# The S5 mixer of a two-layer trunk in straight line: paired gelu, tables prepared earlier, first gated columns in native fp32

## The chip, the cores and the metric

The kernel runs on one core of a Trainium2 chip. The metric is the device time of one execution in microseconds; the median of several runs counts.

## The reference, cut to what matters

Two layers over 256 tokens of 2048 channels. Layer 0 is differential attention and an MLP with squared ReLU, layer 1 an S5 state space mixer with a gated output (GLU), and an MLP; a norm ends it. Only the S5 mixer is touched, and the last two matrix products of the first MLP run beside steps that are moved.

```python
def s5_mixer(h, ...):                      # h: rmsnorm(x) * gain, 256 x 2048
    u = h.reshape(B, S, S5_GROUPS, S5_GROUP)
    bu_re = einsum('sgc,gpc->sgp', u_s, bb_re); bu_im = ...
    x_re, x_im = associative_scan(_scan_combine, (a_re, a_im, bu_re, bu_im))
    y = einsum('sgp,gcp->sgc', x_re, cr) - einsum('sgp,gcp->sgc', x_im, ci)
    y = y + d_skip * h
    g = gelu(y)
    val, gate = split(g @ w_glu, 2, axis=-1)    # w_glu: 2048 x 4096
    return val * sigmoid(gate)
```

## The kernel before, in words

All matrix products with weights run on TensorE in the fp32r type, with both operands split in two parts: `wh` is the weight cast by ScalarE (`prep`, L173), `wl` the remainder by VectorE or GpSimd (L99, L178, L179), and each product takes three matmuls, h x h, h x l, l x h (L186 to L188, `ktile`). Weights come in chunks of 512 KB (two 128-deep slices, 512 columns) on the queue of SyncE (SP), `load`, five buffers (`raw`); `prep` of chunk i also loads chunk i + 5. An output block is 512 columns wide and takes eight chunks.

Side work is written as generators. `pump` advances every generator that is due, once after each 128-deep slice of a main matrix product; `spawn` adds one. The order in which the Python code issues is the order of each engine's queue; the engines wait for one another by semaphores. A tile with a tag takes the buffer of that tag that was freed first.

The S5 mixer works on 16 tiles of 128 channels, four tokens to a chunk, so that a tile has 4 x 64 columns. Per tile j there is a table in DRAM, `scr[j]`, 1.5 MB, made from the weights beside the first layer (`s5_pre`), and these steps:

- `s5_u` (two tiles): TensorE transposes the residual (L940), ScalarE copies it in 16 pieces of 32x128 into u (L945); `s5_scale` multiplies by the norm's factor per token (L951, GpSimd; VectorE for the first pair).
- `s5_fetch`: three loads of 512 KB, `te`, `to` and `t` (L926 to L928), for j < 3 on SP's queue, after that on ScalarE's, and a copy of the decay `rr` on ScalarE (L930).
- `s5_e`: state inputs, 16 fp32 matmuls (32 records in the trace, L961), then a chain on VectorE: two multiplications by the turn, an add and a subtraction, two scans (L971), two multiplications back, a subtraction for the real half; the add for the imaginary half runs on GpSimd for j < 10 (L983).
- `s5_y`: outputs, 24 fp32 matmuls (48 records, L994), then 16 gelus of 32x64 on ScalarE (L999).
- `s5_split`: the cast of the gelu's result (ScalarE, L1010) and the remainder (L1011, GpSimd for j < 10).

`s5_run` is the generator that issues them, tile after tile, with `keep_warm` matmuls that nobody reads (L269) at its start. The main stream meanwhile multiplies the first 512 columns of value and gate (`a_v`, `a_g`, `gemm_block`): per tile twelve fp32r matmuls of 512 columns, as soon as the tile is split. Chunks 384 to 399 (GLU0 = 384) are those weights; they are cast and split like all the others. Then follow the other three column blocks, `gemm(glu_lhs)`. `early_u` makes u of tiles 0 to 3 and fetches tables 0 and 1 beside the last three products of the first MLP; `done0` starts it after the first of four last products, and `gemm_skewed` is the last of them.

Of the kernel before, what the change touches and what calls it, by code (L numbers as in the profile page):

```python
# [16 lines left out]
P = 128  # L17
S = 256
# [38 lines left out]
def tile_trunk(  # L57
# [104 lines left out]

    def prep(i):
        if i >= len(stream) or i in preps:
            return
# [5 lines left out]
        for k in range(0, WK, step):  # L171
            sl = slice(k, k + step)
            act.copy(h[:, sl], r[:, sl])  # L173
            if FINE <= i < POOL or GLU0 <= i < GLU0 + 16:
                if i < GLU0 or i >= GLU0 + 2:
                    sub(l[:, 0], r[:, 0], h[:, 0].bitcast(F32))
                else:
                    pool_e.tensor_tensor(out=l[:, 0], in0=r[:, 0], in1=h[:, 0].bitcast(F32), op=ALU.subtract)  # L178
# [15 lines left out]
    def gemm_block(accs, lhs, first, last, ks=range(KB)):  # L194
        """accumulate one weight block (512 deep, 512 wide) or a part of it for both token tiles"""
# [22 lines left out]
    def gemm_t(lhs_blocks):  # L218
        """as gemm, but the result transposed: weights stationary, tokens moving"""
# [22 lines left out]
    def gemm_skewed(lhs_blocks, done):  # L242
        """the last half of the depth one token tile after the other"""
# [19 lines left out]
    def keep_warm(n):  # L263
        """matmuls whose result nobody reads: TensorE's clock drops when it idles"""
# [86 lines left out]
    class Norm:  # L351
        """rms statistics of the residual, a block of columns at a time"""
# [15 lines left out]
        def finish(self, ts=slice(0, NT)):  # L368
            """1/sqrt(mean square + eps), or its square"""
# [78 lines left out]
    def evict_qk(hp, accs, which):  # L448
        """queries unscaled (their norm factor enters the softmax), keys with theirs"""
# [9 lines left out]
    def head(hp, hh):  # L459
        """scores, softmax, difference; waits for v; values, sub-norm, transposed output"""  # L460
# [117 lines left out]
    def s5_pre():  # L578
# [10 lines left out]
        # lambda and step in the layout [(group of pair, state), pair]  # L589
# [660 lines left out]
```

## Time and profile before

| | us |
|---|---|
| median of 3 runs | 2154.13 (2153.45 to 2154.57) |
| profiled execution, span from first to last instruction | 2150.9 |
| TensorE busy | 2098.5 (98%) |
| VectorE busy | 1340.2 (62%) |
| ScalarE busy | 1088.6 (51%) |
| GpSimd busy | 178.3 (8%) |

Of the profiled execution only the span is given; its time is not among the three. PE is TensorE, PEld its weight loads, DVE VectorE, ACT ScalarE, POOL GpSimd, SP SyncE. A busy TensorE is not TensorE at its peak, and matmul records overlap: spacing of starts says more than durations. A native fp32 matmul leaves two records.

### The profile page before, as it was taken

Reading aid. Unit: us, or ns where it says so; the run is one execution under the profiler, and the core shown is the slowest. Engines: PE = TensorE matmul, PEld = TensorE weight load, DVE = VectorE, ACT = ScalarE, POOL = GpSimd, SP = SyncE. Lnnn points to the kernel's source line nnn. Section 1 sums busy time; section 2 is a strip of 40 time slices with the busy share of each in tenths; the row PEclk is TensorE's granted clock in tenths of the full one; section 3 lists DMA queues with packets and bytes.
Section 4 is the critical chain, followed back from the end, with each engine's and each line's share of the span. In section 5 each row is a group of like instructions: output and inputs, shape, how many; then the busy total and the mean of one; then the engine's idle time right before and its main releaser. Section 6 shows DMA issues by size and latency. Waiting matters only on the chain.

```text
span 2150.9 us, 35993 instructions
## 1 busy us (share of the span) xinstructions
PE 2098.5 (98%) x14210; PEld 1887.1 (88%) x14210; DVE 1340.2 (62%) x2182; ACT 1088.6 (51%) x1685; POOL 178.3 (8%) x279
## 2 busy tenths in 40 slices
PE   8999999999999999999997789999999999999998
PEld 8899988898899899889975568899889989989986
DVE  5775556777677767757766775555555555545555
ACT  5444545555444544544465995454434434434443
POOL 1000200120021012001102520000000000000000
PEclk9999999999999999999999899999999999999999
DMA  7567765788777778776776755666566566566653
GB/s 243 157 199 234 240 182 175 221 235 279 222 233 231 267 223 233 273 238 220 229 248 224 264 183 182 195 197 191 190 193 183 187 194 186 176 199 184 191 191 127
DMA packets 230829, 452.83 MB, mean 211 GB/s; under 512 B 20818, under 2 KB 29348, under 8 KB 230660
## 3 DMA queue, kind: packets, MB, share of 16 engines
q1 hardware_dynamic: 212784, 395.89, 58.9%
q0 software_dynamic: 11440, 32.86, 4.7%
q10 hardware_dynamic: 6436, 21.79, 2.8%
q8 instruction: 111, 1.82, 0.3%
q14 instruction: 58, 0.48, 0.1%
HBM read 420.85 MB, written 41.68 MB: 215 GB/s over the span
## 4 chain that ended last, share of the span: by engine, by line
PE 92%; ACT 3%; DVE 2%; DMA 1%; issue 1%; ACTq 0%; POOL 0%; SPq 0%; DVEq 0%; POOLq 0%
PE acc L186 15%; PE acc L188 15%; PE acc L187 15%; PE acc L233 14%; PE acc L234 14%; PE acc L235 14%; ACT s2k L999 1%; ACT vsb L945 1%; ACT wh L173 1%; PE sd L388 0%; DVE wl L99 0%; DVE c L93 0%; PE sd L961 0%; PE sd L994 0%; DVE s2k L971 0%
## 5 line engine op out<-in xcount | busy, mean ns | idle before, releaser
L99 DVE TENSOR_TENSOR wl<-raw,wh 128x1024 fp32r<-128x1024 f32 (+1 forms) x704 | 851.6, 1215 | 657.3 <-ACT wh L173 651.5
L173 ACT CAST wh<-raw 128x1024 fp32r<-128x1024 f32 (+1 forms) x706 | 735.6, 1046 | 768.5 <-PE acc L188 384.7
L233 PE MATMUL acc<-xh,wh 128*128 128x256 f32 x1536 | 439.9, 286 | 1.2 <-ACT wh L173 1.2
L235 PE MATMUL acc<-xh,wl 128*128 128x256 f32 x1536 | 435.3, 283 | 0.0
L234 PE MATMUL acc<-xl,wh 128*128 128x256 f32 x1536 | 435.3, 283 | 0.0
L186 PE MATMUL acc<-wh,xh 128*128 128x512 f32 x896 | 357.2, 399 | 23.1 <-ACT xh L1010 20.4
L187 PE MATMUL acc<-wl,xh 128*128 128x512 f32 x896 | 352.0, 393 | 0.8 <-POOL wl L178 0.8
L188 PE MATMUL acc<-wh,xl 128*128 128x512 f32 x896 | 352.1, 393 | 0.4 <-DVE xl L1011 0.4
L233 PEld LDWEIGHTS acc<-xh,wh 128*128 128x128 f32 x1536 | 295.3, 192 | 3.4 <-ACT wh L173 1.6
L234 PEld LDWEIGHTS acc<-xl,wh 128*128 128x128 f32 x1536 | 295.4, 192 | 0.4
L235 PEld LDWEIGHTS acc<-xh,wl 128*128 128x128 f32 x1536 | 295.3, 192 | 0.2 <-DVE wl L99 0.2
L233 PE MATMUL acc<-ah,wh 128*128 128x256 f32 x1024 | 289.9, 283 | 0.0
L235 PE MATMUL acc<-ah,wl 128*128 128x256 f32 x1024 | 289.8, 283 | 0.0
L234 PE MATMUL acc<-al,wh 128*128 128x256 f32 x1024 | 289.8, 283 | 0.0
L186 PE MATMUL acc<-wh,ah 128*128 128x512 f32 x640 | 251.6, 393 | 0.4 <-ACT wh L173 0.4
L187 PE MATMUL acc<-wl,ah 128*128 128x512 f32 x640 | 249.4, 390 | 1.4 <-DVE wl L99 1.4
L188 PE MATMUL acc<-wh,al 128*128 128x512 f32 x640 | 249.3, 390 | 0.0
L186 PEld LDWEIGHTS acc<-wh,xh 128*128 128x128 f32 x896 | 169.7, 189 | 58.7 <-ACT xh L1010 21.5
L188 PEld LDWEIGHTS acc<-wh,xl 128*128 128x128 f32 x896 | 169.7, 189 | 38.0 <-POOL bc L980 1.2
L187 PEld LDWEIGHTS acc<-wl,xh 128*128 128x128 f32 x896 | 170.1, 190 | 35.0 <-POOL wl L178 1.2
L234 PEld LDWEIGHTS acc<-al,wh 128*128 128x128 f32 x1024 | 196.6, 192 | 0.2
L233 PEld LDWEIGHTS acc<-ah,wh 128*128 128x128 f32 x1024 | 196.6, 192 | 0.2
(237 smaller groups left out, 1931.6 us busy)
## 6 DMA issues: line engine op xcount, KB each, us to landing
raw<-in_mlp_w_dram SPq DMA_DIRECT2D x512, 512.0 KB
raw<-in_a_w_in_dram SPq DMA_DIRECT2D x94, 512.0 KB
raw<-in_b_w_glu_dram SPq DMA_DIRECT2D x64, 512.0 KB
raw<-in_a_w_out_dram SPq DMA_DIRECT2D x32, 512.0 KB
scr<-t POOLq DMA_DIRECT2D x32, 512.0 KB, 6.0
te<-scr ACTq DMA_DIRECT2D x13, 512.0 KB
to<-scr ACTq DMA_DIRECT2D x13, 512.0 KB
t<-scr ACTq DMA_DIRECT2D x13, 512.0 KB
```

The lines of the kernel that those rows point to most:

```text
L99: v.tensor_tensor(out=o, in0=a, in1=b, op=ALU.subtract)
L173: act.copy(h[:, sl], r[:, sl])
L186: pe.matmul(accs[t], lhs.h[:, k, ts], wh, start=first, stop=False)
L187: pe.matmul(accs[t], lhs.h[:, k, ts], wl, start=False, stop=False)
L188: pe.matmul(accs[t], lhs.l[:, k, ts], wh, start=False, stop=last)
L233: pe.matmul(o, wh[:, kk, cs], lhs.h[:, k], start=f and c % 2 == 0, stop=False)
L234: pe.matmul(o, wh[:, kk, cs], lhs.l[:, k], start=False, stop=False)
L235: pe.matmul(o, wl[:, kk, cs], lhs.h[:, k], start=False, stop=e and c % 2 == 1)
L945: act.copy(u[32 * s:32 * s + 32, :, q], pv[32 * q:32 * q + 32, :, L - 1 - s])
L999: act.activation(gv[32 * q:32 * q + 32, s], py[32 * s:32 * s + 32, q], AF.Gelu_apprx_tanh)
```

## The change

`s5_run`, a generator, becomes `s5_phase`, a straight loop over the 16 tiles; the interleaver runs only the table generator beside it. In iteration j it issues the state inputs of tile j + 1, a decay row of tile j + 3 (now a GpSimd copy, `s5_dk`), a scaling, the GLU step of tile j - 3 (`glu_tile`), the outputs of tile j and, at the end of a pair, 16 gelus of 32x128 for both tiles with one split (`s5_y` over a group; the last two tiles are alone), u of a pair (tiles 8 to 15 only), and the fetch of table j + 4. `glu_tile` multiplies the unsplit gelu by the raw weights, four native fp32 matmuls of 512 columns per tile, so chunks 384 to 399 are not cast nor split. All tables are fetched on SP's queue. The add of the imaginary half and the remainder are on GpSimd for all tiles. u of tiles 4 to 7 is made in the first MLP, after its second last-quarter product, and `early_tables` fetches tables from there as soon as `s5_pre` is done. Comments are removed elsewhere.

```diff
-S5_POOL = 10
+LAG = 3
     def prep(i):
-        if i >= len(stream) or i in preps:
+        if i >= len(stream) or i in preps or GLU0 <= i < GLU0 + 16:
             return
...
-        load(i + RAW)
+        load_next()
...
     def s5_fetch(j):
-        eng = nc.sync if j < 3 else nc.scalar
-        te = lp.tile([P, 2, Q, P], F32, tag="ah", name=nm("te"))
+        tag = "x" if j < 3 else "a"
+        te = lp.tile([P, 2, Q, P], F32, tag=tag + "h", name=nm("te"))
...
+    def s5_dk(j):
+        dk = tmp([P, Q, NCH], "s1k", bufs=4)
+        pool_e.tensor_copy(dk, rr[:, j * Q:(j + 1) * Q, None].broadcast_to([P, Q, NCH]))
...
+    def s5_y(grp):
...
         for s in range(L):
             for q in range(Q):
-                act.activation(gv[32 * q:32 * q + 32, s], py[32 * s:32 * s + 32, q], AF.Gelu_apprx_tanh)
+                act.activation(gv[32 * q:32 * q + 32, 0:n, s], py[32 * s:32 * s + 32, 0:n, q], AF.Gelu_apprx_tanh)
+        act.copy(blk.h[:, kk:kk + n], g[:, 0:n])
+        pool_e.tensor_tensor(out=blk.l[:, kk:kk + n], in0=g[:, 0:n], in1=blk.h[:, kk:kk + n].bitcast(F32), op=ALU.subtract)
...
+    def glu_tile(j):
+        g = G.pop(j)
+        c, kk = GLU0 + j // WK * 2, j % WK
+        for i, accs in ((c, a_v), (c + 1, a_g)):
+            for t in range(NT):
+                pe.matmul(accs[t], g[:, t * P:(t + 1) * P], raws[i][:, kk], start=j == 0, stop=j == NJ - 1)
+            if j == NJ - 1 and i == c:
+                first_vals.extend(evict_val(a_v))
+            if kk == WK - 1:
+                load_next()
+                pos[0] += 1
+
+    def s5_phase(norm):
+        until(lambda: norm.done)
         keep_warm(WARM[0])
...
         s5_scale(0, rsb, v)
+        for j in range(3):
+            DK[j] = s5_dk(j)
         s5_scale(2, rsb)
         s5_e(0)
+        keep_warm(WARM[2])
...
         for j in range(NJ):
+            if j + 1 < NJ:
+                s5_e(j + 1)
+            if j + 3 < NJ:
+                DK[j + 3] = s5_dk(j + 3)
+            if j % 2 == 0 and j + 4 < NJ and j + 4 in U:
                 s5_scale(j + 4, rsb)
+            if j >= LAG:
+                glu_tile(j - LAG)
+            gen, end = ys[j]
+            next(gen)
...
+            if j % 2 == 1 and j + 7 < NJ:
+                s5_u(j + 7)
+            s5_fetch(j + 4)
+            pump()
+        for j in range(NJ - LAG, NJ):
+            prep(GLU0 + 16 + j - NJ + LAG)
+            glu_tile(j)
...
+        if u < 2:
+            spawn(early_u(u), 4)
         if u == 0:
-            spawn(early_u(), 4)
+            spawn(early_tables(), 2)
...
+    def early_u(u):
+        for j in (4 * u, 4 * u + 2):
+            s5_u(j)
+            yield 4
+
+    def early_tables():
+        while "done" not in s5:
             yield 1
+        for j in range(4):
+            s5_fetch(j)
+            yield 8
+            while j == 2 and pos[0] < last_mlp0 - 2:
+                yield 1
```

## Rows read from the trace of the kernel before

**Rows 1.** Timeline, TensorE: start us, us, engine line op out<-in xcount [idle before].
```profile
1139.79 0.39 PE L188 MATMUL acc<-wh,al 128*128 128x512 f32 x1
1140.02 4.24 PE L269 MATMUL acc<-xh 128*128 128x512 f32 x18
...
1287.19 0.39 PE L186 MATMUL acc<-wh,xh 128*128 128x512 f32 x1
1287.41 0.39 PE L187 MATMUL acc<-wl,xh 128*128 128x512 f32 x1
```
**Rows 2.** Stretches: from:to, us, then each engine's busy us, clock, DMA share, GB/s.
```profile
1160.00:1170.00 10.00, 3.87 (x87) 3.15 (x83) 8.16 (x14) 9.57 (x32) 3.48 (x5) 1.00 0.59 187
1170.00:1180.00 10.00, 5.15 (x55) 3.78 (x55) 6.29 (x9) 9.58 (x35) 3.71 (x6) 0.71 0.56 187
1171.00:1182.30 11.30, 7.18 (x59) 4.98 (x59) 6.22 (x10) 10.94 (x34) 4.80 (x8) 0.65 0.57 189
1182.30:1196.00 13.70, 11.63 (x183) 9.48 (x182) 13.16 (x17) 13.01 (x44) 10.18 (x12) 0.92 0.88 299
1190.00:1285.00 95.00, 75.77 (x1004) 57.90 (x1001) 72.27 (x120) 89.55 (x289) 34.76 (x47) 0.93 0.65 221
```
**Rows 3.** Chain of waits from 1070 to 1300, its shares by line.
```profile
by line: ACT s2k L999 13.2%; PE acc L186 11.3%; PE acc L188 10.7%; PE acc L187 10.5%; ACT vsb L945 10.0%; issue 8.0%; ACT wh L173 3.5%; DVE c L93 3.4%; PE sd L961 3.3%; PE sd L994 3.2%; DVE s2k L971 3.2%; DVE s2k L93 3.0%; DMA t<-bbr 2.8%; 
```
**Rows 4.** Groups of ScalarE from 1140 to 1287, by form: busy us, mean ns, idle before.
```profile
L999 ACT ACTIVATE s2k<-sd 32x64 f32<-32x64 f32 x256 | 71.5, 279 | 11.9 <-PE sd L994 8.8
L945 ACT COPY vsb<-sd 32x128 f32<-32x128 f32 x96 | 24.7, 257 | 1.2
L173 ACT CAST wh<-raw 128x1024 fp32r<-128x1024 f32 x19 | 19.6, 1043 | 0.0
L1010 ACT CAST xh<-s2k 128x256 fp32r<-128x256 f32 x16 | 6.5, 405 | 0.4
L930 ACT COPY s1k<-rr 128x256 f32<-128x256 f32 x14 | 5.6, 400 | 3.0 <-PE sd L1025 2.8 <-issue 0.2
```
**Rows 5.** Timeline of ScalarE, the same step of two pairs of tiles.
```profile
1223.30 4.66 ACT L999 ACTIVATE s2k<-sd 32x64 f32<-32x64 f32 x16
...
1240.31 4.64 ACT L999 ACTIVATE s2k<-sd 32x64 f32<-32x64 f32 x16
```
**Rows 6.** Timeline of TensorE at an attention head: native fp32, 256 columns.
```profile
90.53 0.60 PE L512 MATMUL sd<-vsb,s2k 128*128 128x256 f32 x2
90.96 0.59 PE L513 MATMUL sd<-vsb,s2k 128*128 128x256 f32 x2
91.39 0.59 PE L514 MATMUL sd<-vsb,s2k 128*128 128x256 f32 x2
```
**Rows 7.** Timeline and chain: state inputs and outputs of S5 on TensorE.
```profile
1145.94 2.08 PE L961 MATMUL sd<-vsb,te 128*64 128x64 f32 x64
1154.70 1.15 PE L961 MATMUL sd<-vsb,te 128*64 128x64 f32 x32
1182.33 1.98 PE L961 MATMUL sd<-vsb,te 128*64 128x64 f32 x32
1255.38 1.55 PE sd L994 x48
```
**Rows 8.** Timeline of VectorE and GpSimd, the first tiles of S5.
```profile
1147.13 1.29 DVE L93 TENSOR_TENSOR c<-sd,t 128x512 f32<-128x512 f32 x2 [1.29 <-PE sd L961]
1152.08 1.28 DVE L93 TENSOR_TENSOR c<-sd,t 128x512 f32<-128x512 f32 x2
1157.02 1.28 DVE L93 TENSOR_TENSOR c<-sd,t 128x512 f32<-128x512 f32 x2
1161.96 1.28 DVE L93 TENSOR_TENSOR c<-sd,t 128x512 f32<-128x512 f32 x2
1163.29 1.54 POOL L951 TENSOR_TENSOR vsb<-vsb,rsb 128x512 f32<-128x512 f32 x1 [0.66 <-ACT vsb L945]
1163.62 1.50 DVE L99 TENSOR_TENSOR c<-c 128x256 f32<-128x256 f32 x1
1165.04 1.26 DVE L971 TENSOR_TENSOR_SCAN s2k<-s1k,c 128x256 f32<-128x256 f32 x2
```
**Rows 9.** Groups of GpSimd and VectorE from 1140 to 1287, by form.
```profile
L951 POOL TENSOR_TENSOR vsb<-vsb,rsb 128x512 f32<-128x512 f32 x7 | 10.6, 1517 | 20.4 <-DVE rsb L1027 19.8 <-ACT vsb L945 0.7
L983 POOL TENSOR_TENSOR bc<-s2k,s2k 128x252 f32<-128x252 f32 x10 | 9.2, 916 | 18.2 <-DVE s2k L93 18.2
L1011 POOL TENSOR_TENSOR xl<-s2k,xh 128x256 fp32r<-128x256 f32 x10 | 8.2, 817 | 39.4 <-ACT xh L1010 39.4
...
L971 DVE TENSOR_TENSOR_SCAN s2k<-s1k,c 128x256 f32<-128x256 f32 x32 | 23.3, 767 | 0.0
```
**Rows 10.** A stretch of the first MLP in which tables 0 and 1 are loaded.
```profile
1126.00:1137.00 11.00, 11.00 (x50) 9.13 (x49) 3.99 (x9) 2.83 (x4) 0.00 (x0) 1.00 0.98 374
```
**Rows 11.** Timeline of TensorE in the first MLP, where u of tiles 0 to 3 is made.
```profile
1086.23 0.50 PE L186 MATMUL acc<-wh,ah 128*128 128x512 f32 x1 [0.36 <-ACT wh L173]
1087.49 0.50 PE L187 MATMUL acc<-wl,ah 128*128 128x512 f32 x1 [0.76 <-DVE wl L99]
...
1093.83 0.50 PE L187 MATMUL acc<-wl,ah 128*128 128x512 f32 x1 [0.60 <-DVE wl L99]
```

More of the change, by code (lines that the diff above doesn't have):

```diff
@@ L173, in prep @@
             act.copy(h[:, sl], r[:, sl])
[L174 to L178, printed above, removed]
+            if FINE <= i < POOL:
+                sub(l[:, 0], r[:, 0], h[:, 0].bitcast(F32))
                 pool_e.tensor_tensor(out=l[:, 1], in0=r[:, 1], in1=h[:, 1].bitcast(F32), op=ALU.subtract)
@@ L980, in s5_e @@
         pool_e.memset(xp[:, :, :, 0:1], 0.0)
-        eng = pool_e if j < S5_POOL else v
         sub(xp[:, 0, :, 1:], w1[:, 0, :, 0:n], w2[:, 1, :, 0:n])
-        eng.tensor_tensor(out=xp[:, 1, :, 1:], in0=w1[:, 1, :, 0:n], in1=w2[:, 0, :, 0:n], op=ALU.add)
+        pool_e.tensor_tensor(out=xp[:, 1, :, 1:], in0=w1[:, 1, :, 0:n], in1=w2[:, 0, :, 0:n], op=ALU.add)
         X[j] = xp
-    def s5_y(j):
-        te, to, tt, ct, dk = tab.pop(j)
-        u, xp = U.pop(j), X.pop(j)
-        py = bank()[:, 0:Q * NCH].rearrange("p (q k) -> p q k", q=Q)
-        for q in range(Q):
-            terms = ((tt[:, q], u[:, q]), (to[:, 0, q], xp[:, 0, q]), (to[:, 1, q], xp[:, 1, q]))
-            for n, (m, d) in enumerate(terms):
-                for h in (slice(0, GP), slice(GP, P)):
-                    pe.matmul(py[h, q], m[:, h], d, start=n == 0, stop=n == 2)
-        g = tmp([P, S], "s2k", bufs=7)
-        gv = g.rearrange("p (k s) -> p s k", s=L)
+    def s5_y(grp):
+        n = len(grp)
+        py = bank().rearrange("p (j q k) -> p j q k", j=2, q=Q)
+        for jj, j in enumerate(grp):
+            te, to, tt, ct = tab[j]
+            u, xp = U[j], X[j]
+            for q in range(Q):
+                terms = ((tt[:, q], u[:, q]), (to[:, 0, q], xp[:, 0, q]), (to[:, 1, q], xp[:, 1, q]))
+                for m, (w_, d) in enumerate(terms):
+                    for h in (slice(0, GP), slice(GP, P)):
+                        pe.matmul(py[h, jj, q], w_[:, h], d, start=m == 0, stop=m == 2)
+            yield j
+            del U[j], X[j], tab[j]
+        g = tmp([P, 2, S], "s2k", bufs=7)
+        gv = g.rearrange("p j (k s) -> p j s k", s=L)
@@ L997, in s5_y @@
         for s in range(L):
             for q in range(Q):
[L999 to L1005 removed]
+                act.activation(gv[32 * q:32 * q + 32, 0:n, s], py[32 * s:32 * s + 32, 0:n, q], AF.Gelu_apprx_tanh)
+        blk, kk = glu_lhs[grp[0] // KB], grp[0] % KB
         if blk.h is None:
             new_lhs(blk, "x")
[L1008 to L1014 removed]
@@ L1016, in s5_run @@
-    def s5_run(norm):
-        while not norm.done:
-            yield 1
+        act.copy(blk.h[:, kk:kk + n], g[:, 0:n])
+        pool_e.tensor_tensor(out=blk.l[:, kk:kk + n], in0=g[:, 0:n], in1=blk.h[:, kk:kk + n].bitcast(F32), op=ALU.subtract)
+        if kk + n == KB:
+            blk.ready = True
+        for jj, j in enumerate(grp):
+            G[j] = g[:, jj]
+    def glu_tile(j):
+        g = G.pop(j)
+        c, kk = GLU0 + j // WK * 2, j % WK
[7 more added lines that the diff above has]
+                pos[0] += 1
@@ L1179, in tile_trunk @@
     a_v, a_g = new_accs(), new_accs()
-    for b in range(NB):
-        for k in range(0, KB, WK):
-            ks = range(k, k + WK)
-            gemm_block(a_v, glu_lhs[b], b == 0, b == NB - 1, ks)
-            if b == NB - 1 and ks.stop == KB:
-                vs = evict_val(a_v)
-            gemm_block(a_g, glu_lhs[b], b == 0, b == NB - 1, ks)
-    evict_gate(a_g, vs, 0)
+    s5_phase(norm2)
+    evict_gate(a_g, first_vals, 0)
     for u in range(1, NB):
```

71 lines of the change are left out of this document (23 added, 48 removed).

## The prediction

> **What bounds the kernel now.** I read the page first: TensorE is busy for 98% of the span and nearly every slice is full, so the place to look is the one where the slices are not full. That is the S5 stage between the two MLPs. The timeline dates it: the last matmul of the first MLP starts at 1139.79, the 18 warming matmuls at 1140.02, and the second column block of the GLU (its matmuls then run without a break) at 1287.19 [rows 1]. The stage lasts 1287.2 - 1140.0 = **147.2 us**. The stretches show why: from 1160 on ScalarE is busy for 0.94 to 0.96 of every stretch, while TensorE falls to 0.4 or 0.5 in places and its granted clock to 0.65 [rows 2]. The chain of waits for 1070 to 1300 puts 13.2% on the gelu and 10.0% on the copies of u, both ScalarE [rows 3]. The groups of ScalarE in the stage say what it does: 256 gelus of 279 ns, 96 copies of 257 ns, 19 casts of weights of 1043 ns, 16 casts and 14 table rows of about 400 ns [rows 4]. Its timeline repeats every 17.0 us (gelu runs at 1223.30 and 1240.31) [rows 5], two tiles of channels at a time: 8.5 us per tile, against about 5.3 us of TensorE work. ScalarE sets the stage; that is what is to be replaced.
>
> **The change, part by part.** I lay out the new program order and ask at each point which engine is late.
>
> *ScalarE.* A pair of tiles now shares 16 gelus of 32x128. No row has that shape: it costs at least the 279 ns of 32x64, at most twice that. Casts grow from 405 ns (256 columns) to 1043 ns (1024), 0.83 ns a column [rows 4], so I take 0.279 + 64 x 0.00083 = 0.332 us, 5.3 us a pair; the copy of u with 128 columns at 257 ns says the same. Add one split copy of 512 columns (0.63 by the same slope) and, for the four pairs whose u is still made here, 4.1 us. A pair costs 10.0 us at most, 5.9 later. The eight 1043 ns weight casts per four pairs, the table rows and the table issues leave ScalarE. It stops being the bound if anything else needs over 5 us per tile.
>
> *TensorE.* The old GLU step is 12 matmuls at a spacing of 0.227 us [rows 1], 2.7 us per tile. The new one is four native fp32 matmuls of 512 columns. The trace has native fp32 of 256 columns: starts at 90.53, 90.96, 91.39, two records each, so 0.43 us [rows 6]. With 512 columns I estimate 0.86 and 3.44 us per tile: 0.7 more than before, bought against the casts. The other work per tile: the state inputs 1.05 us (32 records; two tiles of 64 in 2.08) and the outputs 1.5 us (48 records in 1.55) [rows 7]. An iteration is 3.44 + 1.05 + 1.5 = **6.0 us**, with 0.45 more where four transposes for u are made (iterations 1, 3, 5, 7).
>
> *VectorE.* With little beside it, its chain per tile has a period of 4.94 us (1147.13, 1152.08, 1157.02, 1161.96) [rows 8]. It loses the weights' remainders. It now shares with a fuller GpSimd: two adds of 0.92, a row copy for each tile (not in the trace on GpSimd; between ScalarE's 0.40 for the same copy and GpSimd's 0.82 for two inputs of that size, taken as 0.6), one scaling of 1.3 to 1.5, one 512-wide remainder of about 1.3 [rows 8, 9]. What that does to VectorE is in the rows: the 0.42 us subtraction at 1163.62 took 1.50 beside GpSimd's scaling at 1163.29, and the scan began 1.1 us late [rows 8]. One such block per tile gives 6.0 us; none gives 4.94. I take 5.8, from the nearer stretch with a loaded GpSimd, so VectorE is just beneath TensorE. A new wait sits on GpSimd: the remainder of a pair waits for its gelu and split, 6 us after the pair's outputs, and the add of the tile after next is queued behind it, ready some 8.6 us after those outputs (6.0 + 1.3 + 0.9 and hand-overs). TensorE wants it after transposes, two state inputs, two GLU steps and one output, 0.45 + 2.1 + 6.9 + 1.5 = 10.9 us: 2 us of cover, costed at nothing; without it each pair loses what is missing.
>
> The rule that speaks against this change is the Trainium skill's, SBUF — State Buffer, section "Who interferes with whom": a VectorE instruction with two SBUF inputs contends with a GpSimd instruction that reads SBUF, and the second fully blocks until the first ends. The trace agrees at 1163.62, where the subtraction ended as the scaling did plus its own 0.4; it is the first rival below.
>
> *DMA.* Per iteration a table of 1.57 MB and on average one weight chunk of 0.52 MB: 2.1 MB. In 1126 to 1137 the queues moved 374 GB/s at 0.98 busy [rows 10]: 5.6 us, under 6.0. All tables now go through SP's queue, where the fetch of table j+4 waits for the outputs of tile j, and the weight loads queue behind it; weights are five chunks ahead, and a table has two iterations (12 us) until its use, so I cost that at nothing. Without that cover each late table costs its lateness once. Tables 0 to 2 and u of tiles 4 to 7 move into the last two GEMMs of the first MLP (table 3 is asked for there too, but by the order of its steps I read its fetch as falling into iteration 0). The transposes there cost 2 x 0.45 us of a full TensorE. The same two steps for tiles 0 to 3 in the GEMM before left waits of 0.36, 0.76 and 0.60 us on weight casts and remainders [rows 11]; bounds 0 and 1.7, taken 0.7. **MLP: +1.6 us.**
>
> *Start.* State inputs of tile 0, the warming matmuls and the first outputs stay where they are. Outputs of tile 1 come after its add at about 1157.7. In iteration 0 GpSimd also copies a row and scales u, so tile 2 gets the 1.1 us delay above: its outputs end near 1165.1. The gelu of the first pair (1158.9 + 5.3 + split) is then ready. GLU steps run three tiles behind, so the first one opens iteration 3 at about 1165.1, **25.1 us** after the stage's start.
>
> *Steady run.* Iterations 3 to 15: 13 x 6.0, less 1.05 (no state inputs after tile 15), plus 3 x 0.45 for transposes: **78.3 us**. *Tail:* three GLU steps, **10.3 us**, the last gelu (4.5 us) under the first two. The next GEMM's three chunks are cast there by an otherwise idle ScalarE.
>
> **Sum.** 25.1 + 78.3 + 10.3 = 113.7 against 147.2: -33.5, and +1.6 in the MLP: -31.9. I add 0.15 us per iteration for hand-overs between engines that both need about 6 us: +2.0. That leaves -29.9. The profiled span is 2150.9, and the three runs around it 2153.45 to 2154.57: 3.2 us lie around the span at the median of 2154.13. So the span should be 2121.0 and the time 2154.1 - 29.9 = **2124 us**.
>
> **Rivals.**
> *VectorE becomes the bound.* If both a scaling or remainder and a row copy block it in each tile, it needs 4.94 + (1.4 + 1.3) / 2 + 0.6 = 6.9 us. From 1157.0, fourteen tiles take 96.6 us, then come outputs (1.5), the tail (10.3) and the MLP's 1.6: an end at 1267 where the forecast has 1140.0 + 113.7 + 1.6 + 2.0 = 1257.3: **2134**. For it: VectorE's mean scan of 767 ns against 630 undisturbed [rows 8, 9]. Against it: adds fall under multiplications from PSUM, which were not slowed at 1161.96.
> *TensorE's clock stays as uneven as now.* Before the first GLU step TensorE works 2.5 of every 4.95 us; in the old stage it then fell to 1.2 GHz, 65% granted from 1171 to 1182, and state inputs took 1.98 us instead of 1.15 [rows 2, 7]. At a mean of 0.85, an iteration is 7.06: +13.8, **2138**. Against it: the new program leaves no idle microseconds after iteration 3, and in the old one the clock came back at full work (0.92 from 1182).
> *Tables come late.* At the 299 GB/s of 1182 to 1196 [rows 2] the 2.1 MB take 7.0 us in eight iterations: +8, **2132**. Or the paired gelu saves nothing (0.558 us each): 13.6 us per pair in the first four, +1.6 each: **2131**, that is, it doesn't do what it says.
> *Slower.* Native fp32 at the lower level throughout: GLU step 6.9, iteration 12.0, tail 20.6; the stage takes 25 + 156 + 21, near 202: **2210**. It decides from an iteration of 8.5 us on (147.2 - 1.6 - 25.1 - 10.3, over 13), that is if 40% of the work ran at 1.2 GHz. A TensorE that is never idle at that level speaks against it.
>
> **How the numbers follow.** Forecast (2118 to 2128): 0.52. VectorE: 0.16. Clock: 0.14. Tables 0.09, gelu 0.03, slower 0.04, and 0.02 for less than 2118 (no hand-over loss, no MLP stall, tile 2 not delayed). The range for 8 in 10 reaches from **2114** (the sum with all unknown costs at their low ends and a shorter start) to **2142** (clock rival with some hand-over loss). A measurement of this kernel can tell about 0.2%, 4 us, from no change. All but the slower rival and a twin of it near the point of decision are faster by more: faster 0.94, same 0.02, slower 0.04.
>
> **What would show it.** Right: ScalarE's busy share in the stage near 0.65, native matmul pairs of two records at 0.43 us each, GLU steps of four at a period of about 6.1 us, VectorE at 0.95, granted clock 1.0 from 1170 on, the second column block starting near 1257 to 1258. Wrong: TensorE waiting for the add or GpSimd in each iteration (VectorE rival), records of 0.85 us (clock), waits on table tiles (DMA), or native matmuls whose spacing does not double from 256 to 512 columns.

## The result, and the profile after

| | before | after |
|---|---|---|
| median of runs, us | 2154.35 (2153.45 to 2155.26, 4 runs) | 2127.13 (2125.83 to 2128.56, 4 runs) |
| ratio | | 0.9874, interval 0.9860 to 0.9888 |
| profiled span, us | 2150.9 | 2125.4 |
| end of the first MLP, us | 1140.02 | 1142.39 |
| second column block begins, us | 1287.19 | 1260.76 |
| S5 stage between them, us | 147.2 | 118.4 |

The change makes the kernel 27.2 us faster by the medians, 25.5 by the two profiled spans. The forecast was 2124, with a range of 2114 to 2142: the sign and the mechanism held, and the gain was forecast 3 us too large. The span divides into three parts: the MLP became 2.4 us longer, the stage 28.8 shorter, and what follows the stage 0.9 longer (864.64 instead of 863.71 us from the second column block to the end).

The stretches of the stage after the change (columns as in [rows 2]: busy us of TensorE, its weight loads, VectorE, ScalarE, GpSimd; then granted clock, DMA share, GB/s):

```profile
1154.00:1166.00 12.00, 8.11 (x168) 7.06 (x168) 11.76 (x22) 3.88 (x8) 4.62 (x9) 0.86 0.63 220
1166.00:1180.00 14.00, 12.38 (x172) 7.97 (x172) 13.76 (x24) 13.13 (x39) 6.14 (x13) 1.00 0.56 193
1180.00:1200.00 20.00, 20.00 (x282) 12.56 (x282) 17.07 (x27) 17.61 (x55) 9.26 (x17) 1.00 0.91 308
1200.00:1220.00 20.00, 20.00 (x304) 12.96 (x302) 17.94 (x31) 16.55 (x47) 6.73 (x13) 1.00 0.95 331
1220.00:1240.00 20.00, 20.00 (x313) 13.09 (x310) 18.10 (x30) 9.75 (x24) 9.31 (x17) 1.00 0.71 258
```

From 1180 to 1240 TensorE is busy for all 60 us at the full granted clock, where before it was busy for 0.80 of 1190 to 1285 at a mean clock of 0.93 [rows 2]. The stage has changed its owner, from ScalarE to TensorE: ScalarE's 0.94 to 0.96 is now 0.49 to 0.88 there, and VectorE is at 0.85 to 0.91. What holes remain in these rows lie before 1180.

The timeline of TensorE, from the start of the stage to its end (columns as in [rows 1]; a value in brackets is the idle time ahead of the instruction and what ended it):

```profile
1142.39 4.24 PE L270 MATMUL acc<-xh 128*128 128x512 f32 x18
...
1162.94 1.81 PE L968 MATMUL sd<-vsb,te 128*64 128x64 f32 x32
...
1167.29 1.10 PE L968 MATMUL sd<-vsb,te 128*64 128x64 f32 x32
1169.94 3.70 PE L1027 MATMUL acc<-raw,s2k 128*128 128x512 f32 x8 [1.55 <-ACT s2k L1010]
...
1182.97 3.70 PE L1027 MATMUL acc<-raw,s2k 128*128 128x512 f32 x8
...
1189.81 3.70 PE L1027 MATMUL acc<-raw,s2k 128*128 128x512 f32 x8
...
1196.01 3.70 PE L1027 MATMUL acc<-raw,s2k 128*128 128x512 f32 x8
...
1245.49 3.70 PE L1027 MATMUL acc<-raw,s2k 128*128 128x512 f32 x8 [0.59 <-ACT s2k L1010]
...
1250.67 10.57 PE L1027 MATMUL acc<-raw,s2k 128*128 128x512 f32 x24
1260.76 0.71 PE L187 MATMUL acc<-wh,xh 128*128 128x512 f32 x1
```

L1027 is the native fp32 GLU step: 8 records in 3.70 us, and 24 records from 1250.67 to 1260.76, 0.42 each. L1003 are the outputs, L968 the state inputs; the transposes for u (0.6 us) lie between the two. The state inputs at 1162.94 take 1.81 us instead of 1.10, in the stretch whose clock is 0.86. An iteration without transposes takes 6.2 us (1189.81 to 1196.01) and one with them 6.84 (1182.97 to 1189.81). Iteration 3 opens at 1167.29 with state inputs, 24.9 us after the start; then TensorE waits 1.55 us for the gelu.

ScalarE's groups from 1142 to 1261 by form (columns as in [rows 4], which they answer):

```profile
L1010 ACT ACTIVATE s2k<-sd 32x128 f32<-32x128 f32 x112 | 44.8, 400 | 16.2 <-PE sd L1003 10.4 <-issue 4.6
L952 ACT COPY vsb<-sd 32x128 f32<-32x128 f32 x64 | 16.4, 256 | 0.8
L1010 ACT ACTIVATE s2k<-sd 32x64 f32<-32x64 f32 x32 | 8.8, 276 | 0.4
...
L1010 ACT ACT_TABLE_LOAD x1 | 1.3, 1283 | 17.9 <-PE sd L1003 17.9
```

The paired gelu takes 400 ns, not the 332 of the prediction, and a load of the gelu's table, 1.28 us, stands ahead of the first of them, after ScalarE had been idle for 17.9 us. (The Trainium skill, page ScalarE: Activation LUTs, section "What ACT_TABLE_LOAD costs", gives about 1283 ns for the load instruction, and the trace agrees: 1283.)

The last two matrix products of the first MLP, where u of tiles 4 to 7 is now made (timeline of TensorE, to be read beside [rows 11]):

```profile
1101.35 0.60 PE L947 MATMUL sd<-ident,xres 128*128 128x128 f32 x4
...
1116.70 0.50 PE L187 MATMUL acc<-wh,ah 128*128 128x512 f32 x1 [0.65 <-ACT wh L177]
1117.97 0.51 PE L188 MATMUL acc<-wl,ah 128*128 128x512 f32 x1 [0.76 <-DVE wl L99]
```

And behind the stage, transposes of the residual for the second MLP's input:

```profile
1264.70 0.30 PE L389 MATMUL sd<-ident,xres 128*128 128x128 f32 x1 [0.71 <-DVE xres L96]
...
1265.93 0.55 PE L389 MATMUL sd<-ident,xres 128*128 128x128 f32 x3 [0.94 <-DVE xres L96]
```

These are the two small costs: 0.65 + 0.76 us of waits for split weights in the MLP beside 0.9 of transposes, and two waits of 1.65 together where the kernel before had one of 0.74.

### The profile page after: what moved, and what is told of

Its sections match the earlier page's. It is cut to its first block, busy times and chain, and to the rows that moved or that the text cites. A ratio compares the mean times of both kernels' runs of the same rounds, so it can differ in the third digit from the quotient of the medians.

```text
span 2125.4 us, 35656 instructions
## 1 busy us (share of the span) xinstructions
PE 2097.5 (99%) x14146; PEld 1871.7 (88%) x14146; DVE 1323.8 (62%) x2156; ACT 1048.4 (49%) x1534; POOL 166.3 (8%) x282
## 4 chain that ended last, share of the span: by engine, by line
PE 94%; ACT 2%; DVE 2%; DMA 1%; issue 1%; SPq 0%; POOL 0%; ACTq 0%; DVEq 0%
PE acc L187 15%; PE acc L188 15%; PE acc L189 15%; PE acc L234 15%; PE acc L236 14%; PE acc L235 14%; PE acc L1027 2%; PE sd L1003 1%; ACT s2k L1010 1%; ACT wh L177 1%; PE sd L968 1%; DVE wl L99 1%; ACT vsb L952 1%; PE sd L389 1%; PE sd L470 0%
## 5 line engine op out<-in xcount | busy, mean ns | idle before, releaser
L99 DVE TENSOR_TENSOR wl<-raw,wh 128x1024 fp32r<-128x1024 f32 (+1 forms) x690 | 837.0, 1219 | 660.6 <-ACT wh L177 655.0
L177 ACT CAST wh<-raw 128x1024 fp32r<-128x1024 f32 (+1 forms) x690 | 718.7, 1046 | 771.3 <-PE acc L189 382.2
L187 PE MATMUL acc<-wh,xh 128*128 128x512 f32 x832 | 326.9, 393 | 0.0
L189 PE MATMUL acc<-wh,xl 128*128 128x512 f32 x832 | 324.2, 390 | 0.0
L188 PE MATMUL acc<-wl,xh 128*128 128x512 f32 x832 | 324.2, 390 | 0.0
L236 PEld LDWEIGHTS acc<-ah,wl 128*128 128x128 f32 x1024 | 196.7, 192 | 0.0
L189 PEld LDWEIGHTS acc<-wh,xl 128*128 128x128 f32 x832 | 156.2, 188 | 32.7
L187 PEld LDWEIGHTS acc<-wh,xh 128*128 128x128 f32 x832 | 156.3, 188 | 32.2 <-ACT vsb L1198 0.4
```

Of the source, the lines that this page charges most:

```text
L99: v.tensor_tensor(out=o, in0=a, in1=b, op=ALU.subtract)
L187: pe.matmul(accs[t], lhs.h[:, k, ts], wh, start=first, stop=False)
L188: pe.matmul(accs[t], lhs.h[:, k, ts], wl, start=False, stop=False)
L189: pe.matmul(accs[t], lhs.l[:, k, ts], wh, start=False, stop=last)
L236: pe.matmul(o, wl[:, kk, cs], lhs.h[:, k], start=False, stop=e and c % 2 == 1)
```

## The experiments

Times are compared with the kernel before in runs on the same chip; its medians there were 2152.2 to 2153.9, where the result above has 2154.35, so a difference of 1 to 2 us between kernels that ran on different chips says little. "Against before" is the difference of the two medians; for the change itself it is -27.2.

**1. The old gelu in the new order.** Every tile has its own 16 gelus and its own split.

```diff
-        groups = [(0, 1), (2, 3), (4, 5), (6, 7), (8, 9), (10, 11), (12, 13), (14,), (15,)]
+        groups = [(j,) for j in range(NJ)]
```

> The changed kernel (2127.1 us) with its gelu for single tiles again: 32 gelus of 32x64 a pair instead of 16 of 32x128, nothing else. Theory (ScalarE's work made the old stage, its removal made the gain): ScalarE then needs 9.3 + 0.8 + 4.3 = 14.4 us per pair while u is still made (four pairs), against 12.4 us of the loop now, so 2 us are lost four times, less up to 3 us because the first GLU step no longer waits for a paired gelu: 2130 to 2135. Rival (the straight order of issue made the gain, not less work): unchanged, 2127.

Measured: 2129.99 us (2129.14 to 2131.82), ratio 0.9893 (0.9878 to 0.9908), -23.0 against before. Pairing is worth some 3 to 4 us; the stage is 121.9 us long here and 118.4 in the change. ScalarE is busy for 0.93 to 0.96 of the stretches from 1180 to 1240, and TensorE waits for gelus twice, 3.5 us together, so ScalarE is at its limit again without the pairs. One of these stretches, and the first of the two waits on TensorE's timeline:

```profile
1200.00:1220.00 20.00, 18.50 (x260) 11.48 (x261) 15.40 (x27) 19.10 (x70) 6.64 (x14) 1.00 0.89 306
```

```profile
1177.99 1.86 PE L968 MATMUL sd<-vsb,te 128*64 128x64 f32 x32 [2.01 <-ACT s2k L1010]
```

**2. The old split products in the new order.** The GLU steps use cast and split weights and the split gelu, as before, with the remainders made half on VectorE and half on GpSimd; the casts stand at the step that comes just ahead of their use.

```diff
-        if i >= len(stream) or i in preps or GLU0 <= i < GLU0 + 16:
+        if i >= len(stream) or i in preps:
...
-                pe.matmul(accs[t], g[:, t * P:(t + 1) * P], raws[i][:, kk], start=j == 0, stop=j == NJ - 1)
+                ktile(accs, blk, j % KB, wh[:, kk], wl[:, kk], t, j == 0, j == NJ - 1)
...
+            if j >= 1:
+                prep(GLU0 + j - 1)
```

> The changed kernel with the first gated columns multiplied in two parts again: chunks 384 to 399 are cast on ScalarE (1.04 us each, one per tile), split half on VectorE and half on GpSimd, and a GLU step is twelve fp32r matmuls. Theory: TensorE gets 0.8 us per tile cheaper, yet ScalarE needs 13.6 us a pair and VectorE, with 0.7 us more of its own and 1.3 to 1.5 us more of GpSimd in its way per tile, some 7 us per tile: 2135 to 2147. Rival (order made the gain, and TensorE is what bounds): TensorE's 0.8 us come off in each of 13 iterations and three tail steps, 2115.

Measured: 2156.81 us (2154.39 to 2158.09), ratio 1.0015 (1.0006 to 1.0025): outside what was expected, and as slow as the kernel before. Timelines of TensorE and ScalarE in this run:

```profile
1211.84 0.50 PE L187 MATMUL acc<-wh,xh 128*128 128x512 f32 x1 [2.82 <-ACT wh L177]
```

```profile
1206.45 4.27 ACT L952 COPY vsb<-sd 32x128 f32<-32x128 f32 x16
1210.74 1.99 ACT L177 CAST wh<-raw 128x1024 fp32r<-128x1024 f32 x2
1217.18 6.55 ACT L1010 ACTIVATE s2k<-sd 32x128 f32<-32x128 f32 x16 [4.44 <-PE sd L1003]
```

ScalarE is not full (it idles 4.44 us), but the casts (1210.74) stand in its order behind the gelus, the split and u, and TensorE waits 2.82 us for them; then ScalarE waits for TensorE's outputs. A pair of tiles takes 17.96 us: the same wait of 2.82 stands at 1229.80. TensorE's granted clock is 0.77 to 0.91 in the stretches from 1166 to 1260. That is a loop of two engines that wait for each other, which I had not foreseen: part of the price is the place of the casts and not their work. Run 4 tells how much.

**3. Both: single gelus and split products**, so that nearly the order of the program alone is new. The edits are those of 1 and 2.

> Both undone together: single gelus and the split weights, with the straight loop, the early tables and early u kept. It separates the order from the work. Theory: the work on ScalarE is back at 16.5 us a pair for four pairs and 12 later, VectorE at 7 us and more per tile: 2143 to 2153, most of the gain gone. Rival (order): 2115 to 2127.

Measured: 2147.04 us (2145.38 to 2147.36), ratio 0.9970 (0.9959 to 0.9982), -5.9 against before. With the casts where they stand in 2, the order alone is worth 6 of the 27 us. TensorE waits 2.6 to 2.8 us a pair for casts here too, so the same order with earlier casts might be worth more; that kernel wasn't run. Against 2, which differs from this one by the pairs alone, this kernel is 9.8 us faster: beside split products pairing was a loss.

**4. As 2, with the casts one iteration earlier**, to tell their place from their work.

```diff
-            if j >= 1:
-                prep(GLU0 + j - 1)
+            prep(GLU0 + j)
```

> The split weights of e2 (2156.8 us), but each chunk is cast one iteration earlier, ahead of the pair's gelu in ScalarE's order. In e2 the trace has the two casts behind gelu, split copy and u of a pair, and the GLU step waiting 2.8 us for them once a pair: part of e2's time is where I put the casts. Theory (work): VectorE's some 7 us a tile and ScalarE's 13.6 us a pair remain: 2136 to 2146. If the place was all of it: near 2120.

Measured: 2148.04 us (2145.73 to 2150.47), ratio 0.9974 (0.9963 to 0.9984), -5.9 against before: slower than either end of what was expected. The place of the casts was worth some 9 us (2156.81 to 2148.04), and some 21 us to the change remain. The waits for casts are gone, and two others have come. Once, TensorE waits long for a table (its timeline):

```profile
1171.54 1.98 PE L968 MATMUL sd<-vsb,te 128*64 128x64 f32 x32 [9.34 <-DMA te<-scr]
```

And VectorE is now full, 19.5 to 19.7 of 20 us in each stretch from 1180 to 1260, with a pair at 14.9 us (gelu runs at 1196.22, 1211.11 and 1226.02). One of its groups from 1200 to 1240 (busy us, mean ns):

```profile
L99 DVE TENSOR_TENSOR c<-c 128x256 f32<-128x256 f32 x5 | 7.5, 1502 | 0.0
```

This subtraction takes 0.42 us alone; it takes 1.50 beside one of GpSimd's remainders, of the gelu or of the weights (1.46 us, at 1204.29 and 1211.73). VectorE makes the other half of the weights' remainders, at 1.21 us each. So both rivals of the prediction that name VectorE and late tables came true in this kernel, though not in the change. Why the table was late wasn't tried; the split weights' loads stand in the same queue.

**5. Native fp32 alone in the old order.** The kernel before, with its own gelus, its own order and its own table fetches, but GLU steps on raw weights.

```diff
-        if i >= len(stream) or i in preps:
+        if i >= len(stream) or i in preps or GLU0 <= i < GLU0 + 16:
...
-            gemm_block(a_v, glu_lhs[b], b == 0, b == NB - 1, ks)
...
+                        pe.matmul(accs[t], GL[j][:, t * P:(t + 1) * P], raws[i][:, kk % WK], start=j == 0, stop=j == NJ - 1)
```

> The kernel before (about 2154 us) with one part of the change alone: the first gated columns multiplied in native fp32 from the raw chunks, 16 casts and remainders gone, all else as before (generator, single gelus, u and tables late). Theory (ScalarE's work): 16 casts of 1.04 us leave the engine that bounds, 16.6 us, and some are given back at the end where the next chunks are cast: 2137 to 2143. Rival (native fp32 is dearer on TensorE, 0.8 us in 16 tiles, so it gives nothing by itself): 2150 to 2156.

Measured: 2143.12 us (2141.68 to 2145.05), ratio 0.9949 (0.9934 to 0.9964), -10.8 against before, at the upper edge of what was expected. ScalarE's timeline shows what is left of its period: gelu runs at

```profile
1200.49 4.67 ACT L999 ACTIVATE s2k<-sd 32x64 f32<-32x64 f32 x16
...
1216.28 4.66 ACT L999 ACTIVATE s2k<-sd 32x64 f32<-32x64 f32 x16
```

15.8 us per pair instead of 17.0 [rows 5]. The product that is dearer for TensorE (3.4 instead of 2.7 us a tile, by the spacing of the matmuls) is cheaper for the kernel, since ScalarE, busy for 0.91 to 0.96 of 1180 to 1240, and not TensorE sets this loop. The edit takes the remainders off VectorE and GpSimd as well, and no run parts these from the casts. Native products alone give 10.8, the order alone (3) 5.9, and both without pairing (1) 23.0, which is 6.3 more than their sum. The parts do not add: what one is worth depends on the others, and pairing is a gain of some 4 beside native products and a loss of 9.8 beside split ones.

**6. What is the next bound behind TensorE?** The gate's GLU matmuls of tiles 1 to 14 are left out, some 24 us of TensorE work (14 tiles at 1.72).

```diff
-            for t in range(NT):
+            for t in range(NT if accs is a_v or j in (0, NJ - 1) else 0):
```

> The changed kernel without the gate's matmuls of tiles 1 to 14 in the first columns (that part of the computation is left out), so a GLU step has two native matmuls, 1.75 us less. It asks what stands behind TensorE in the loop. Theory: TensorE's 6.1 us per iteration are the bound with VectorE close behind, 4.95 us in odd and about 6.5 us in even iterations, mean 5.7: the loop gains only 0.4 us in 13 iterations and the tail some 3.5 us, 2117 to 2120. If VectorE already is the bound: only the tail, 2123. If VectorE is not near: 1.75 us in 13 iterations and the tail, about 2101.

Measured: 2120.92 us (2119.76 to 2123.05), ratio 0.9851 (0.9836 to 0.9866): 6 us for 24 of work, just outside the 2117 to 2120 of the theory. VectorE is busy for 18.5 to 19.6 of 20 us, which I read as showing that it is the next bound.

**7. The same without GpSimd's scaling**, to test that reading. The first kernel here leaves only the scalings in the loop out, the second also the gate's matmuls as in 6.

```diff
-                s5_scale(j + 4, rsb)
+                U[j + 4], U[j + 5] = U[j + 4][:, 0], U[j + 4][:, 1]
```

> The change, with GpSimd's six scalings of u in the loop left out (tiles 4 to 15 are then computed from an unscaled u). If GpSimd's scaling slows VectorE's scans (2.34 instead of 1.27 us a pair) and VectorE then holds up TensorE, periods of iteration fall from 6.1 to 6.85 us to the TensorE work of 6.0 to 6.45, and the run takes 2123 to 2125. If TensorE alone sets the loop, the scans are faster and the time is within 1 us of the changed kernel's 2127. Either way the scan pairs should take 1.3 us wherever no other GpSimd operation runs beside them.

> The scalings of u in the loop left out, and the gate's GLU matmuls of tiles 1 to 14 as well, so that TensorE isn't the bound. Compared with the run that leaves out only the gate's matmuls (2120.9, pairs of tiles at 11.5 us, VectorE busy for 0.97 of a stretch). If VectorE is the second bound by way of the scaling, pairs fall to about 10.5 us where ScalarE has no u left to copy; while it still copies u, its own 11.3 us a pair (16 gelus of 0.41, 16 copies of 0.26, a split of 0.63) keep them at 11.3. That gives two or three pairs at 1 us: 2118 to 2120. If the add, the row copies and the remainders are what slows VectorE, nothing changes: 2120 to 2122.

Measured: 2127.18 us (2126.91 to 2129.36), ratio 0.9887 (0.9870 to 0.9903), and 2121.08 us (2119.61 to 2123.35), ratio 0.9856 (0.9841 to 0.9871). By the medians neither is faster than its counterpart. Yet VectorE was relieved. Its scans from 1180 to 1240 (busy us, mean ns), first in the change, then with the scalings left out:

```profile
L978 DVE TENSOR_TENSOR_SCAN s2k<-s1k,c 128x256 f32<-128x256 f32 x19 | 16.7, 916 | 0.0
L93 DVE TENSOR_TENSOR c<-sd,t 128x512 f32<-128x512 f32 x19 | 12.3, 686 | 5.9 <-PE sd L968 5.9
```

```profile
L978 DVE TENSOR_TENSOR_SCAN s2k<-s1k,c 128x256 f32<-128x256 f32 x19 | 12.4, 692 | 0.0
L93 DVE TENSOR_TENSOR c<-sd,t 128x512 f32<-128x512 f32 x19 | 12.3, 687 | 10.2 <-PE sd L968 10.2
```

The 4.3 us that the scans gave back went into VectorE's wait for TensorE's state inputs, which grew from 5.9 to 10.2. So VectorE did not hold TensorE up in the change. In the second kernel it isn't the next bound either. Its timelines of TensorE and of ScalarE:

```profile
1184.12 1.98 PE L1027 MATMUL acc<-raw,s2k 128*128 128x512 f32 x4
...
1194.55 1.15 PE L968 MATMUL sd<-vsb,te 128*64 128x64 f32 x32 [1.77 <-ACT s2k L1010]
1195.64 1.98 PE L1027 MATMUL acc<-raw,s2k 128*128 128x512 f32 x4
...
1217.65 1.98 PE L1027 MATMUL acc<-raw,s2k 128*128 128x512 f32 x4 [1.62 <-ACT s2k L1010]
...
1228.61 1.98 PE L1027 MATMUL acc<-raw,s2k 128*128 128x512 f32 x4 [1.38 <-ACT s2k L1010]
```

```profile
1199.47 6.56 ACT L1010 ACTIVATE s2k<-sd 32x128 f32<-32x128 f32 x16
...
1206.71 4.27 ACT L952 COPY vsb<-sd 32x128 f32<-32x128 f32 x16
1211.01 6.59 ACT L1010 ACTIVATE s2k<-sd 32x128 f32<-32x128 f32 x16
```

While u is copied, ScalarE runs without a gap, 11.5 us a pair, and TensorE's pair has the same 11.5; the kernel of 6 has this period there too, with ScalarE as full. Later the GLU step waits for the paired gelu itself, and a pair takes 10.96 (1217.65 to 1228.61); ScalarE in turn waits 3.74 us a pair for TensorE's outputs there, so this is a loop of the two and not a full engine. Behind TensorE, whose own pair takes 13.0 and later 12.2, stands ScalarE once more. My verdict in 6 fell for all pairs but the last: there TensorE waits 0.99 us for the add that follows VectorE's chain, and the pair takes 11.83 us in the kernel of 6 and 10.93 here. Dated from its own start, the stage was 111.9 us long in 6 and is 109.9 here; the other 1 us lies in a last GLU step that took 5.40 us there and 3.70 here.

**8. u of tiles 4 to 7 at the start of the stage**, where TensorE runs matmuls that nobody reads, and no longer in the MLP.

```diff
-        if u < 2:
+        if u == 0:
             spawn(early_u(u), 4)
...
         s5_e(0)
+        s5_u(4)
+        s5_u(6)
         keep_warm(WARM[2])
```

> The changed kernel, but u of tiles 4 to 7 is made at the start of the stage (after the first state inputs), not in the first MLP. The MLP ended 2.4 us later than in the kernel before; the trace has transposes and two waits for casts (0.65, 0.76 us) there, and ScalarE idle from 1144 to 1162 in the stage. Theory: the 2.4 us come back and nothing is lost: 2124 to 2125.5. Rival (the MLP's delay has another cause, such as the tables loaded there, or the copies delay the stage): 2127 or more.

Measured: 2125.50 us (2122.79 to 2125.78), ratio 0.9863 (0.9847 to 0.9880), at the upper edge of what was expected. The waits at 1116.70 and 1117.97 are gone; the stage, from 1140.86 to 1258.86, is 118.0 us long, no longer than before this edit (118.4). Dated from the first transposes for u (1076.74 in the change, 1078.28 here), the MLP ends after 65.7 us in the change and after 62.6 here; over all kernels of this document it is 64.9 to 67.0 with the four steps in the MLP and 62.5 to 63.4 without them. So moving them there cost 2 to 3 us, and at the start of the stage they cost nothing. The medians (2125.50 and 2127.13) show 1.6 of it, and the intervals of the two ratios overlap.

**9. The same, with the gelu's table loaded at the start too.**

```diff
+        act.activation(warm_act, warm_act, AF.Gelu_apprx_tanh)
         keep_warm(WARM[0])
```

> The change, with u of tiles 4 to 7 made at the start of the stage instead of in the first MLP, and the gelu table loaded there too, before it is needed. Only the second edit is new against the run with u at the start (2125.5). Theory: the 1.28 us table load stands on the path to the first GLU step, so this is 1 to 1.5 us faster than that run: 2124.0 to 2124.8, with the first GLU step about 1.3 us earlier. Rival: the table load is covered, because TensorE waits at that point for VectorE's chain or loses the same time later: 2125.2 to 2126.

Measured: 2125.63 us (2124.80 to 2125.81), ratio 0.9875 (0.9861 to 0.9890): no gain, as the rival had it. The wait for the gelu is gone, and the stretch shows what took its place (the window, then TensorE's timeline):

```profile
1164.00:1168.00 4.00, 3.67 (x72) 3.52 (x74) 3.93 (x9) 3.85 (x11) 1.55 (x4) 0.57 0.61 210
```

```profile
1141.19 4.24 PE L270 MATMUL acc<-xh 128*128 128x512 f32 x18
...
1164.28 1.01 PE L1003 MATMUL sd<-bc,to 128*64 128x64 f32 x8 [2.18 <-issue]
...
1165.29 0.64 PE L1003 MATMUL sd<-bc,to 128*64 128x64 f32 x8
...
1168.24 3.70 PE L1027 MATMUL acc<-raw,s2k 128*128 128x512 f32 x8
```

After a wait of 2.18 us TensorE's clock was granted at 0.57 for this stretch, and eight output records took 0.64 us instead of 0.40. The first GLU step came 27.05 us after the stage's start, with the table on the path 27.11 (run 8).

**10. The same, with matmuls in TensorE's two waits.**

```diff
+            if j in (1, 2):
+                for _ in range(2):
+                    pe.matmul(a_v[0], ident, raws[GLU0][:, 0], start=True, stop=True)
             if j >= LAG:
                 glu_tile(j - LAG)
```

> The run with u at the start and the gelu table loaded early (2125.6), with two native fp32 matmuls of 512 columns that nobody reads, 1.7 us, put ahead of the outputs in iterations 1 and 2, where TensorE waited 1.98 and 2.18 us for GpSimd's add. In that run the granted clock was 0.57 from 1164 to 1168, and the first GLU step came 27.05 us after the stage's start, as late as with the table on the path (27.11). Theory: the gain of the table was taken back by the clock, which fell after TensorE's waits. Then the records of the outputs of tile 2 and of the state inputs of tile 3 take 0.34 to 0.41 and 1.10 us again, the first GLU step comes 25.9 to 26.3 us after the stage's start, and the time is 2124.4 to 2125. Rival: the clock falls somewhere in this stretch whatever TensorE does in it; then it is again below 0.95 in a stretch of 4 us between 1152 and 1168, and the first GLU step comes at 26.8 us or later: 2125.4 to 2126.5.

Measured: 2123.49 us (2122.06 to 2124.36), ratio 0.9865 (0.9849 to 0.9882), -29.0 against before. The median is the lowest of all kernels here that compute the whole result. Against before it is 1.8 us under the change's -27.2, and the intervals of the two ratios overlap. The same window and timeline:

```profile
1164.00:1168.00 4.00, 4.00 (x66) 2.74 (x61) 3.97 (x6) 3.84 (x12) 1.53 (x2) 1.00 0.70 188
```

```profile
1139.78 4.24 PE L270 MATMUL acc<-xh 128*128 128x512 f32 x18
...
1165.63 3.70 PE L1027 MATMUL acc<-raw,s2k 128*128 128x512 f32 x8
```

The clock stays at 1.00, and the first GLU step comes after 25.85 us, with no wait: 1.2 us earlier than in 9, as the theory of the clock said. The stage is 116.7 us long (to 1256.50), 1.4 less than in 9. The median is a further 1 us under what the theory gave; the profiled execution had also reached the end of the MLP 1.4 us earlier, which this edit can't have caused.

**11. An earlier first GLU step**: as 9, but tiles 0 and 1 with single gelus and their GLU steps in iterations 2 and 3, none in iteration 4.

```diff
-        groups = [(0, 1), (2, 3), (4, 5), (6, 7), (8, 9), (10, 11), (12, 13), (14,), (15,)]
+        groups = [(0,), (1,), (2, 3), (4, 5), (6, 7), (8, 9), (10, 11), (12, 13), (14,), (15,)]
...
-            if j >= LAG:
+            if j in (2, 3):
+                glu_tile(j - 2)
+            elif j > 4:
                 glu_tile(j - LAG)
```

> e6 plus three things at the start of the stage: the gelu table is loaded while ScalarE idles (it was loaded at 1162.0, 1.3 us, just ahead of the first gelu), tiles 0 and 1 have gelus of their own, and their GLU steps run in iterations 2 and 3 instead of 3 and 4 (none in 4). Theory (in iterations 0 to 2 the stage waits for VectorE's chain and then 1.55 us for the paired gelu, with TensorE half idle and once at the lower clock): 2119 to 2123. If VectorE's 16 chains bound the whole stage by then: about as e6, 2124.

Measured: 2127.42 us (2126.07 to 2128.76), ratio 0.9875 (0.9861 to 0.9890): a miss, no gain at all. Its timeline of TensorE:

```profile
1161.86 3.70 PE L1027 MATMUL acc<-raw,s2k 128*128 128x512 f32 x8
...
1179.91 1.15 PE L968 MATMUL sd<-vsb,te 128*64 128x64 f32 x32 [3.45 <-ACT s2k L1010]
1180.99 5.40 PE L1027 MATMUL acc<-raw,s2k 128*128 128x512 f32 x8
```

Counted from the stage's start (1139.61), the first step did come earlier, after 22.25 us instead of 27.05 in run 9. But iteration 4 has no GLU step to cover the paired gelu of tiles 2 and 3: the state inputs wait 3.45 us for it (by the code, for the PSUM bank that the gelu reads), the clock falls, and the next step takes 5.40 instead of 3.70 us. That is 5.2 us, and the 4.8 are gone. The second column block begins at 1260.72, 121.1 us after the start, where run 9 has 118.2 (1141.19 to 1259.35). TensorE's outputs of tile 1 also waited 1.26 us, for ScalarE's copies of u. At the third GLU step, which stands in iteration 5 in both kernels, this one is already 1.3 us behind run 9 (41.4 against 40.1 us from the start), and the 1.7 us by which that step is longer make it the 3 us.

## Why the prediction was right, and by how much it was off

Against the span of before the sum said -29.9, and the profile shows -25.5. The time came closer than that (2124 forecast, 2127.1 measured) by luck: the text had taken 3.2 us around the span, while the runs here have 1.7 to 1.9 (the profiled one 2127.24 with a span of 2125.4), and these 1.4 us offset part of the 4.4 us by which the span was too short. The 4.4 us lie in these steps:

- **MLP: +1.6 said, +2.4 measured.** The transposes' 0.9 held; the waits for split weights came to 1.4 (0.65 and 0.76), where I had taken 0.7 between 0 and 1.7. [Rows 11] had shown that very pair of sizes, so the upper bound was the nearer row. Run 8, without these steps in the MLP, does not have this delay.
- **Start: 25.1 said, 24.9 measured** for the opening of iteration 3, in run 8 24.8. VectorE's chain sets it, as the text had it, with one add of 0.42 us held for 1.36 by GpSimd's scaling, at 1160.80. Without the scalings (run 7, first kernel) it is 23.95.
- **Paired gelu: 0.332 us said, 0.400 measured**, mis-sized. The slope of the casts and copies (0.83 ns a column) does not hold for the gelu: from 64 to 128 columns it grows by 124 ns (276 to 400), 1.9 ns a column. A pair takes 6.56 instead of 5.3 us. With the table load of 1.28 us, which no term held, the first gelu is 2.5 us later than I had it, and 1.55 of that stood on the path at the first GLU step; with the table loaded early (run 9) this wait is gone. This is the term that was furthest off.
- **Iteration: 6.0 + 0.15 said, 6.1 to 6.2 measured.** GLU step, outputs and state inputs are as estimated (3.6, 1.5 and 1.1 us with their hand-overs); the native product's spacing doubles from 256 to 512 columns (0.42 a record). Transposes cost 0.6 us, not 0.45. From the opening of iteration 3 to the tail it is 83.4 us where the text had 80.3: 1.55 for the gelu, 0.59 for the last gelu (1245.49), 0.4 for the transposes, and 0.6 that I can't assign.
- **Tail: 10.3 said, 10.1 measured.**
- **Behind the stage: nothing said, +0.9 measured**, the second wait at 1265.93. Run 5 has a single wait there, of 0.94 us, and 863.8 us behind its stage, so the native product alone doesn't bring it; its cause stays open.

Of the rivals: **VectorE** was priced and weighed too high. From 1180 to 1240 it is busy for 53.1 us over 9.5 tiles, 5.6 us a tile, where the rival had 6.9 and the forecast 5.8. Its scans beside GpSimd's scaling do take 2.34 instead of 1.27 us a pair, which these rows of the change show (timelines of VectorE and of GpSimd):

```profile
1198.34 2.34 DVE L978 TENSOR_TENSOR_SCAN s2k<-s1k,c 128x256 f32<-128x256 f32 x2
...
1204.98 1.27 DVE L978 TENSOR_TENSOR_SCAN s2k<-s1k,c 128x256 f32<-128x256 f32 x2
```

```profile
1198.26 1.29 POOL L958 TENSOR_TENSOR vsb<-vsb,rsb 128x512 f32<-128x512 f32 x1
```

The rule of the Trainium skill that spoke against the change (SBUF — State Buffer, section "Who interferes with whom") is thus confirmed in its place, and run 7 shows that the loss lay within VectorE's slack. **The clock** rival decided nothing in the steady run (1.00 from 1166 on), but holds at the start: 0.86 from 1154 to 1166 in the change, and in run 9 a low clock took back 1.2 us. **Late tables** did not occur: no wait of TensorE in the stage is for a DMA, with the queues at 0.91 and 0.95 where all tables and weights pass. **"It doesn't do what it says"** is out: run 1 puts pairing at 3 to 4 us. **The slower rival**, native fp32 at the lower clock throughout, did not occur: the clock is 1.00 from 1166 on. Run 2, back at the time of before at a clock of 0.77 to 0.91, has split products and waits for casts and is no case of it.

What to see in the profile, as said ahead: ScalarE's share of the stage is 0.68 (81.0 of 119 us, said 0.65), the clock 1.00 from 1166 on (said 1170), pairs of records 0.42 a record, iterations 6.1 to 6.2 (said 6.1). Not as said: VectorE at 0.88 of 1180 to 1240, not 0.95, and the second column block 3 us late, at 1260.8.

## What to carry to other kernels

When another engine than TensorE sets a loop, giving TensorE dearer work (3.4 instead of 2.7 us a step) can pay, if it empties the queue of that engine; run 5 showed that for the native products by themselves. Runs 2 and 4 showed that the place of a cast in that queue has a price of its own, some 9 us here. An engine that is busy for 0.98 of a stretch need not be the next bound: take its load away and see whether the time moves, or only its wait. And a wait that is removed ahead of a steady run may be worth nothing if TensorE's clock falls in the gap that is left, as runs 9 and 10 suggest.

## What the runs showed of the hardware that I had not expected

- The cost of a gelu on a small tile grows by 1.9 ns a column (276 ns at 32x64, 400 at 32x128), more than twice the slope of a cast (0.83) on the same engine; a copy of 32x128 takes 256 ns. The Trainium skill (ScalarE: Activation LUTs, section "Step-by-step: what each stage is for") says that all functions cost the same per element, gelu among them; these rows disagree. The gelu here writes every fourth column, which the copy doesn't (it reads every fourth), and whether that or the function makes the difference wasn't tried.
- A wait of 2.18 us on TensorE was followed by a granted clock of 0.57 for the next 4 us in run 9, while the same wait of 2.19 us at the same point of run 8 was not (1.00). With two native products ahead of each of the two waits it stayed at 1.00 in run 10. In the change it was the wait before, 1.98 us at 1159.66, that was followed by 0.63 (1160 to 1164), and runs 8 and 9 have that wait too with 1.00 behind it: a wait of this length was followed by a fall in some executions and not in others. With one profile of each kernel, that the gap's filling is the cause rests on the one pair.
- Profiled executions differ ahead of any edit: the first transposes of the MLP's side work, behind identical work, start between 1075.67 and 1078.46 in the kernels here. A difference of 1 to 2 us between two spans says nothing by itself; the parts of the stage, dated from their own start, do.
